# First loads on the weights' queue, two more split blocks, and a rearranged last store in a two-layer decoder kernel on one Trainium2 core

## The chip, the core and the metric

The kernel runs on one core of one Trainium2 chip. The metric is device time in microseconds (us) of one execution, lower is better. Before the change it took 2313.56 us (median of three runs, 2311.81 to 2315.46).

## What is computed

Two layers of a decoder trunk over 256 positions with a model width of 2048, all in float32. Layer 0 mixes with a chunked gMLP beside a gated linear recurrence, layer 1 with an attention that forgets; each is followed by a gated MLP (5632 hidden columns) with a causal convolution of width 3 between its up-projection and its activation. Cut to what matters:

```python
for l in range(DEPTH):                                   # DEPTH = 2
    h = rms_norm(x, mix_norm[l])
    h = mixer_ab(h, ...) if l % 2 == 0 else mixer_c(h, ...)
    x = x + h
    h = rms_norm(x, ffn_norm[l])
    x = x + conv_ffn(h, ffn_w_up[l], ffn_conv_w[l], ffn_conv_b[l], ffn_w_down[l])
```

Nearly all of the work is matrix products of the 256 positions with weights that are each read once.

## The kernel before, in words

**Layout.** `x` lies feature-major in SBUF: 16 tiles of 128 features by 256 positions (`xT[0..15]`, L69 to L74), held in seven larger tiles named x0, x1, x2, x4, x6, x8 and x12 after their first index, with 1, 1, 2, 2, 2, 4 and 4 tiles in them. The result leaves in the same layout.

**A product.** [...] `weights` (L145) loads a block `w` of 128x1024 by a DMA on the queue of SyncE (SP), ScalarE (ACT) rounds it to `wh` (L162), VectorE (DVE) forms the rest `wl = w - wh` (L165). The activations are split in the same way into a tile `a` that holds both parts side by side (`split`, L272; from x by `Norm.feed_split`, L317: ACT writes the high part, DVE the low one). Each pair of tiles then takes three matmuls: high by high, high by low, low by high. There are four buffers for `w`, three each for `wh` and `wl`, and in the later stages a second pool with two more.

**The start.** Layer 0 begins with `project_tok` (L194) for the columns "v": eight blocks of two k-tiles, 12 matmuls of 128x512 each, fed by the weights in order. Nine small matmuls on a tile of ones come first (L135 to L137). `pp` (norm gains and other small parameters; the first 32 columns are needed at once) and x0 are loaded from ACT's queue, x1, x2, x4 and x6 from the queue of GpSimd (POOL) (L81 to L83), x8 and x12 from SP's queue behind the weights of block k = 6 and k = 8 (`FETCH`, L30). For k = 0 and k = 2 the block is loaded and split in two halves (`single`, L154).

**The ends of the stages.** Products that come out position-major go through `transposed` (L247): DVE turns 32x32 blocks within `tmp`, and 16 small DMAs of 32 KB put the blocks into their places in `zt` or `turn`, eight on SP's queue and eight on POOL's, alternating. There are 80 such batches in the kernel. The consumers of a batch are generators in a queue (`tick`, L121); each block of weights advances them one step, and they first let `LAG` = 4 steps pass (3 for the last quarter). So in `add_four` (L368), in `mixer_c` at the queries and keys (L827, consumed at L758), and in the MLP's `four`/`conv` (L887, L903).

**The last stage.** `down` (L972) of layer 1 makes the output in four quarters. For q = 0, 1 and 2 a quarter goes through `add_y` (L945): transpose, wait, add to x (L954), store each tile from SP's queue (L968). The last quarter is made feature-major, one tile m = 12..15 after the other (L975 to L987), added on DVE (L984, L985) and stored. For m = 15 there is no separate eviction (`end`).

**What sets the order.** The Tile framework schedules instructions onto the engines' in-order queues and gives each DMA one of eight completion semaphores for the hardware queues (SP and ACT together) or one of eight for POOL's; a DMA waits until the one that held its semaphore before has landed. `tc.add_manual_dep(..., order)` fixes an order without a semaphore.

Of the kernel before, what the change touches and what calls it, by code (L numbers as in the profile page):

```python
# [12 lines left out]
ALU = mybir.AluOpType  # L13
AX = mybir.AxisListType

P = 128
# [8 lines left out]
BLK = 32  # L25
LAG = 4
WAIT = 4
EPS = 1e-6
WARM = 9
FETCH = {6: (8,), 8: (12,)}  # L30
LANE = 64
LEVELS = (64, 32, 16, 8, 4, 2, 1)
NL = len(LEVELS)
# [2 lines left out]
C_MIX, C_FFN, C_GAM = 0, 32, 64  # L36
# [14 lines left out]
def tile_trunk(ctx: ExitStack, tc: tile.TileContext, x, pp_d, cst_d, mlev_d, msk_d,  # L51
               w_v, w_f, w_g, w_i, w_q, w_u, w_abo, w_cf, w_cqkv, w_cg, w_co, w_up, w_dn, spw_d, spb_d, out):
    nc = tc.nc
    V, SC, PE = nc.vector, nc.scalar, nc.tensor
# [20 lines left out]
    fetch = {c0: (t, c0, n) for t, c0, n in xload}  # L75
# [12 lines left out]
    order = mybir.DependencyInfo(mybir.DependencyClass.NoSync, mybir.DependencyReason.DATA)  # L88
# [15 lines left out]
    def view(ap, off, *dims):  # L104
        return bass.AP(ap.tensor, ap.offset + off, [list(ap.ap[0])] + [list(d) for d in dims])
# [13 lines left out]
    flight, queue = [], []  # L119
# [15 lines left out]
    warm = pm.tile([P, 512], F32, tag="pm", name="warm")  # L135
    for i in range(WARM):
        PE.matmul(warm[:, 0:P], ones, ones, start=True, stop=True)  # L137
# [2 lines left out]
        while flight or queue:  # L140
            tick()

    deep = {"pool": None, "turn": 0}

    def weights(src, n, rows=None, single=None):  # L145
        deep["turn"] += 1
        if deep["pool"] is not None and deep["turn"] > 12 and deep["turn"] % 2:
            pool, nw, ns = deep["pool"], 2, 2
        else:
            pool, nw, ns = wp, 4, 3  # L150
        w = pool.tile([P, n], F32, tag="w", name=nm("w"), bufs=nw)
        wh = pool.tile([P, n], F32R, tag="wh", name=nm("wh"), bufs=ns)
        wl = pool.tile([P, n], F32R, tag="wl", name=nm("wl"), bufs=ns)
        parts = [slice(i, i + n // 2) for i in (0, n // 2)] if single else [slice(0, n)]  # L154
        for p in parts:
            deep["dma"] = nc.sync.dma_start(
                w[:, p] if rows is None else w.rearrange("p (m c) -> p m c", m=rows), src[:, p] if single else src)
        for i, p in enumerate(parts):
# [3 lines left out]
            deep["act"] = SC.activation(wh[:, p], w[:, p], AF.Copy)  # L162
            if deep["turn"] == 5:
                deep["hold"] = deep["act"]
            V.tensor_tensor(wl[:, p], w[:, p], wh[:, p].bitcast(F32), ALU.subtract)  # L165
        return wh, wl
# [27 lines left out]
    def project_tok(wsrc, norm, feed=False):  # L194
        ps = [pm.tile([P, 512], F32, tag="pm", name=nm("pm")) for _ in range(2)]
        k = 0
        for c in (2,) * 8:
            later = []
            if feed:
                for c0 in FETCH.get(k, ()):  # L200
                    t, c0, n = fetch[c0]
                    later.append((t, c0, n))
                if k >= 4:
                    for i in range(c):
                        norm.feed_split(k + i)
            tick()
            wh, wl = weights(wsrc[:, k * 512:(k + c) * 512], c * 512, single=(norm, k) if feed and k < 4 else None)
            for t, c0, n in later:
                r = nc.sync.dma_start(t, x[:, c0:c0 + n, :])
                tc.add_manual_dep(r.ins, deep["dma"].ins.name, order, reason="queue order")  # L210
            if feed and k < 4:
                for i in range(c):
                    a = norm.a[k + i]
                    for j, (o, t) in enumerate(((0, wh), (S, wh), (0, wl))):
                        for T in range(2):
                            PE.matmul(ps[T], a[:, o + T * P:o + (T + 1) * P], t[:, i * 512:(i + 1) * 512],
                                      start=k + i + j == 0, stop=False)
                k += c
                continue
            for T in range(2):  # L220
                for i in range(c):
                    a = norm.a[k + i]
                    ah, al = a[:, T * P:(T + 1) * P], a[:, S + T * P:S + (T + 1) * P]
                    h, l = (t[:, i * 512:(i + 1) * 512] for t in (wh, wl))
                    PE.matmul(ps[T], ah, h, start=k + i == 0, stop=False)  # L225
                    PE.matmul(ps[T], ah, l, start=False, stop=False)  # L226
                    PE.matmul(ps[T], al, h, start=False, stop=k + i == KT - 1)  # L227
            k += c
        return ps
# [14 lines left out]
                    deep['mm'] = PE.matmul(ps[T], al, h, start=False, stop=k + i == n - 1)  # L244
        return ps

    def transposed(src, tmp, dst):  # L247

        for T in range(2):
            V.transpose(tmp.rearrange("p (b m i t) -> p b m i t", b=4, m=4, t=2)[:, :, :, :, T],  # L250
                        src(T).rearrange("p (m b j) -> p b m j", m=4, b=4))
        n = 2 * BLK
        for a in range(4):
            for b in range(4):
                (nc.sync, nc.gpsimd)[(a + b) % 2].dma_start(dst[BLK * b:BLK * (b + 1), :, a * n:(a + 1) * n],  # L255
                                  tmp[BLK * a:BLK * (a + 1), b * 4 * n:(b + 1) * 4 * n]
                                  .rearrange("p (m r) -> p m r", m=4))

# [616 lines left out]
    def ffn(l, norm, last):  # L875
# [5 lines left out]
        nxt = None if last else Norm(C_MIX + KT)  # L881
# [61 lines left out]
        y = hp.tile([P, 2, D], F32, tag="y", name=nm("y"))  # L943

        def add_y(q, finish):  # L945
            tmp, zt = room()
            transposed(lambda T: y[:, T, q * 512:(q + 1) * 512], tmp, zt)

            def rest():
                for _ in range(LAG - (q == 3)):  # L950
                    yield
                for i in range(4):
                    m = 4 * q + i
                    V.tensor_tensor(xT[m], xT[m], zt[:, i], ALU.add)  # L954
                    if finish:
                        finish_x(m)
                    if q < 3 or i % 2:
                        yield
                if q == 3 and not last:
                    for _ in range(WAIT):  # L960
                        yield
                    yield from nxt.finish_tok()

            queue.append(rest())

        def finish_x(m):
            if last:
                nc.sync.dma_start(out[:, m, :], xT[m])  # L968
            else:
                nxt.feed(m)  # L970

        def down(k0, hid, first, final):  # L972
            n = len(hid)
            for q in range(4):
                if last and final and q == 3:  # L975
                    for m in range(4 * q, KT):
                        end = m == KT - 1
                        ps = project(w_dn[l, m], hid, chunks=(n,), k0=k0, run=2, narrow=end)
                        x2 = xT[m].rearrange("p (n t) -> p n t", t=2)
                        if not end:  # L980
                            t = tp.tile([P, S], F32, tag="ev", name=nm("ev"), bufs=3)
                            SC.activation(t.rearrange("p (n t) -> p n t", t=2),
                                          view(ps, S, (1, P), (P, 2)), AF.Copy)
                            V.tensor_tensor(xT[m], xT[m], t, ALU.add)  # L984
                        V.tensor_tensor(x2, x2, view(ps, 0, (1, P), (P, 2)), ALU.add)  # L985
                        finish_x(m)
                    return  # L987
                ps = project_four(w_dn[l, 4 * q:4 * q + 4], hid, n, k0)
                for T in range(2):
                    d = y[:, T, q * 512:(q + 1) * 512]  # L990
                    if first:
                        SC.activation(d, ps[T], AF.Copy)
                    else:
                        V.tensor_tensor(d, d, ps[T], ALU.add)
                if final:
                    add_y(q, True)

        j0, k0, hid = 0, 0, []
        for g, (now, ahead) in enumerate(STEPS):
# [3 lines left out]
            n, final = 4 * now, g == len(STEPS) - 1  # L1003
# [12 lines left out]
    norm = mixer_ab(Norm(C_MIX))  # L1016
    norm = ffn(0, norm, False)
    norm = mixer_c(norm)
# [81 lines left out]
```

## Time and profile before

| | |
|---|---|
| median of three runs | 2313.56 us |
| lowest, highest | 2311.81, 2315.46 us |
| span of the profiled execution | 2312.9 us (its time is recorded as this span only) |
| TensorE busy, share of the span | 2300.0 us, 99% |
| VectorE, ScalarE, GpSimd busy | 67%, 57%, 15% |
| moved by DMA | 481.44 MB, mean 208 GB/s |

How to read it: the profile is of one execution. PE is the TensorE's matmuls and PEld its weight loads; "SPq", "ACTq" and "POOLq" are the engines' DMA-issuing instructions. In a timeline a row has the start, the duration, the engine and line, the operation with output and input, how many instructions are merged in it, and in brackets how long the engine was idle before it and what ended that. "Issue" means that nothing the profile shows was waited for. Matmuls overlap, so a row's duration exceeds its pitch; what a stall costs is read from start to start. In a table of windows there are, for each engine, the busy time and the instructions that started in the window, then the granted TensorE clock (1.00 is full), the DMA share and GB/s.

### The profile page before, as it was taken

How to read it: one execution, taken by the hardware profiler on the slowest of the kernel's cores; microseconds unless marked ns; L12 is line 12 of the kernel's file. 1: busy time of each engine (PE TensorE's matmuls, PEld its weight loads, DVE VectorE, ACT ScalarE, POOL GpSimd, SP SyncE). 2: the span in 40 equal slices, each digit the busy share in tenths (PEclk: the TensorE clock that was granted, in tenths of full speed). 3: DMA queues.
4: the chain of work that ended last, by engine and by line, in shares of the span. 5: the costliest groups of instructions: out<-in, count | busy, mean ns of one | idle time of the engine just before them, and what ended most of it. 6: DMA issues, size and time to landing. Idle time of an engine off the chain costs nothing.

```text
span 2312.9 us, 31358 instructions
## 1 busy us (share of the span) xinstructions
PE 2300.0 (99%) x10354; PEld 1904.7 (82%) x10354; DVE 1559.5 (67%) x2345; ACT 1307.0 (57%) x1958; POOL 350.4 (15%) x650
## 2 busy tenths in 40 slices
PE   9999999999999999999999999999999999999998
PEld 7888888888888888888888888887888888888887
DVE  7677866776566657766866665666776476667766
ACT  7567655665555546654565556655655465455642
POOL 0100112122012002111211101111221022012102
PEclk9999999999999999999999999999999999999999
DMA  8655577777677767776666655777777677667765
GB/s 274 204 161 173 175 218 220 235 235 212 208 210 207 217 196 212 223 216 186 197 230 194 190 182 178 225 221 227 225 219 216 192 218 209 210 205 213 222 206 166
DMA packets 497748, 481.44 MB, mean 208 GB/s; under 512 B 116288, under 2 KB 468688, under 8 KB 497456
## 3 DMA queue, kind: packets, MB, share of 16 engines
q1 hardware_dynamic: 475488, 453.08, 63.9%
q0 software_dynamic: 20944, 24.04, 4.5%
q10 hardware_dynamic: 1152, 2.31, 0.3%
q8 instruction: 81, 1.33, 0.3%
q14 instruction: 83, 0.68, 0.1%
HBM read 435.24 MB, written 2.11 MB: 189 GB/s over the span
## 4 chain that ended last, share of the span: by engine, by line
PE 95%; DVE 1%; DMA 1%; ACT 1%; issue 1%; POOL 0%; SPq 0%; ACTq 0%; DVEq 0%
PE pm L243 26%; PE pm L244 26%; PE pm L242 26%; PE pm L226 5%; PE pm L227 5%; PE pm L225 5%; DVE wl L165 1%; ACT wh L162 0%; PE px L593 0%; DMA w<-in_w_up 0%; PE pm L186 0%; DMA w<-in_w_v 0%; PE px L762 0%; DMA turn<-tmp 0%; PE px L784 0%
## 5 line engine op out<-in xcount | busy, mean ns | idle before, releaser
L165 DVE TENSOR_TENSOR wl<-w,wh 128x1024 fp32r<-128x1024 f32 (+1 forms) x820 | 998.5, 1220 | 647.2 <-ACT wh L162 639.1
L162 ACT ACTIVATE wh<-w 128x1024 fp32r<-128x1024 f32 (+1 forms) x820 | 864.1, 1056 | 797.2 <-PE pm L244 574.4
L242 PE MATMUL pm<-wh,a 128*128 128x512 f32 x1792 | 699.5, 391 | 1.5 <-ACT wh L162 1.5
L243 PE MATMUL pm<-wl,a 128*128 128x512 f32 x1792 | 699.1, 390 | 1.1 <-DVE wl L165 1.1
L244 PE MATMUL pm<-wh,a 128*128 128x512 f32 x1792 | 698.3, 390 | 0.0
L255 POOL DMA_DIRECT2D zt<-tmp x416 | 225.3, 550 | 1206.8 <-DVE tmp L250 1034.6
L243 PEld LDWEIGHTS pm<-wl,a 128*128 128x128 f32 x1792 | 337.0, 188 | 71.8 <-DVE wl L165 2.7
L242 PEld LDWEIGHTS pm<-wh,a 128*128 128x128 f32 x1792 | 336.7, 188 | 71.2 <-ACT wh L162 1.9
L244 PEld LDWEIGHTS pm<-wh,a 128*128 128x128 f32 x1792 | 336.9, 188 | 69.7
L242 PE MATMUL pm<-wh,hid 128*128 128x512 f32 x688 | 267.6, 389 | 0.0
L243 PE MATMUL pm<-wl,hid 128*128 128x512 f32 x688 | 267.6, 389 | 0.0
L244 PE MATMUL pm<-wh,hid 128*128 128x512 f32 x688 | 267.6, 389 | 0.0
L255 POOL DMA_DIRECT2D turn<-tmp x224 | 121.5, 550 | 739.5 <-DVE tmp L250 332.5
L225 PE MATMUL pm<-wh,a 128*128 128x512 f32 x504 | 199.2, 395 | 0.3 <-ACT wh L162 0.3
L226 PE MATMUL pm<-wl,a 128*128 128x512 f32 x504 | 196.5, 390 | 1.5 <-DVE wl L165 1.5
L227 PE MATMUL pm<-wh,a 128*128 128x512 f32 x504 | 196.5, 390 | 0.0
L244 PEld LDWEIGHTS pm<-wh,hid 128*128 128x128 f32 x688 | 129.1, 188 | 26.9
L243 PEld LDWEIGHTS pm<-wl,hid 128*128 128x128 f32 x688 | 129.1, 188 | 26.8
L242 PEld LDWEIGHTS pm<-wh,hid 128*128 128x128 f32 x688 | 129.1, 188 | 26.8
L226 PEld LDWEIGHTS pm<-wl,a 128*128 128x128 f32 x504 | 94.7, 188 | 21.3 <-DVE wl L165 2.1
L225 PEld LDWEIGHTS pm<-wh,a 128*128 128x128 f32 x504 | 94.7, 188 | 20.0 <-ACT wh L162 1.0
L227 PEld LDWEIGHTS pm<-wh,a 128*128 128x128 f32 x504 | 94.7, 188 | 19.8
(214 smaller groups left out, 1828.7 us busy)
## 6 DMA issues: line engine op xcount, KB each, us to landing
w<-in_w_up SPq DMA_DIRECT2D x352, 512.0 KB, 4.6
w<-in_w_dn SPq DMA_DIRECT2D x176, 512.0 KB, 4.5
w<-in_w_cqkv SPq DMA_DIRECT2D x96, 512.0 KB, 4.4
w<-in_w_abo SPq DMA_DIRECT2D x32, 512.0 KB, 4.8
w<-in_w_cg SPq DMA_DIRECT2D x32, 512.0 KB, 4.4
w<-in_w_co SPq DMA_DIRECT2D x32, 512.0 KB, 4.7
zt<-tmp SPq DMA_DIRECT2D x416, 32.0 KB, 2.8
zt<-tmp POOLq DMA_DIRECT2D x416, 32.0 KB, 2.6
```

The lines of the kernel that those rows point to most:

```text
L162: deep["act"] = SC.activation(wh[:, p], w[:, p], AF.Copy)
L165: V.tensor_tensor(wl[:, p], w[:, p], wh[:, p].bitcast(F32), ALU.subtract)
L225: PE.matmul(ps[T], ah, h, start=k + i == 0, stop=False)
L226: PE.matmul(ps[T], ah, l, start=False, stop=False)
L227: PE.matmul(ps[T], al, h, start=False, stop=k + i == KT - 1)
L242: PE.matmul(ps[T], ah, h, start=k + i == 0, stop=False)
L243: PE.matmul(ps[T], ah, l, start=False, stop=False)
L244: deep['mm'] = PE.matmul(ps[T], al, h, start=False, stop=k + i == n - 1)
L255: (nc.sync, nc.gpsimd)[(a + b) % 2].dma_start(dst[BLK * b:BLK * (b + 1), :, a * n:(a + 1) * n], tmp[BLK * a:BLK * (a + 1), b * 4 * n:(b + ...
```

## The change

1. **Start.** pp goes first on SP's queue, x0 and x1 on ACT's. x2, x4 and x6 go on SP's queue, each ahead of the weights of block k = 2, 4 and 6 (`AHEAD`), x8 and x12 behind the weights of k = 6 and k = 8 (`BEHIND`); `in_order` chains all of these, so that the queue holds them in the order of use. POOL issues none of them.
2. **Halves.** The blocks k = 4 and k = 6 are loaded and split in halves too (eight half blocks in all), with the matmul order of the halves.
3. **Warm-up.** Eight small matmuls instead of nine.
4. **End, transposes.** The 16 small DMAs of the last batch (q = 2) are dealt to three queues, SP 6, ACT 5, POOL 5; they were dealt to SP 8 and POOL 8.
5. **End, adds.** The four adds of that quarter come two steps after their transposes and without steps between them, after an earlier tile's sum; the sum of m = 15 is put behind them.
6. **End, stores.** The tiles are stored in larger pieces: m = 4 and 5 in one transfer and m = 12 to 14 in one transfer from SP's queue, m = 6 and 7, m = 8 to 11 and m = 15 from ACT's. There were 16 stores of 128 KB on SP's queue, now there are nine.

Cut to its core:

```diff
-WARM = 9
-FETCH = {6: (8,), 8: (12,)}
+WARM = 8
+AHEAD = {2: 2, 4: 4, 6: 6}
+BEHIND = {6: 8, 8: 12}
...
-    SC.dma_start(pp[:, 0:C_FFN], pp_d[:, 0:C_FFN])
-    for i, (t, c0, n) in enumerate(xload[:5]):
-        (nc.gpsimd if i else SC).dma_start(t, x[:, c0:c0 + n, :])
+    SC.dma_start(*fetch[0])
+    first_dma = nc.sync.dma_start(pp[:, 0:C_FFN], pp_d[:, 0:C_FFN])
+    SC.dma_start(*fetch[1])
...
+    def in_order(r):
+        tc.add_manual_dep(r.ins, deep["dma"].ins.name, order, reason="queue order")
+        deep["dma"] = r
...
+        for i, p in enumerate(parts):
+            if single and i == 0 and single[1] in AHEAD:
+                in_order(nc.sync.dma_start(*fetch[AHEAD[single[1]]]))
...
-                if k >= 4:
+            if feed and k >= 8:
...
-            wh, wl = weights(wsrc[:, k * 512:(k + c) * 512], c * 512, single=(norm, k) if feed and k < 4 else None)
+            wh, wl = weights(wsrc[:, k * 512:(k + c) * 512], c * 512, single=(norm, k) if feed and k < 8 else None)
+            if feed and k in BEHIND:
+                in_order(nc.sync.dma_start(*fetch[BEHIND[k]]))
...
-                (nc.sync, nc.gpsimd)[(a + b) % 2].dma_start(dst[BLK * b:BLK * (b + 1), :, a * n:(a + 1) * n],
+                qs = queues or (nc.sync, nc.gpsimd)
+                qs[(a + b) % len(qs)].dma_start(dst[BLK * b:BLK * (b + 1), :, a * n:(a + 1) * n],
...
+            end = last and finish and q == 2
+            transposed(lambda T: y[:, T, q * 512:(q + 1) * 512], tmp, zt,
+                       (nc.sync, SC, nc.gpsimd) if end else None)
             def rest():
-                for _ in range(LAG - (q == 3)):
+                for _ in range(2 if end else LAG - (q == 3)):
                     yield
                 for i in range(4):
                     m = 4 * q + i
-                    V.tensor_tensor(xT[m], xT[m], zt[:, i], ALU.add)
+                    r = V.tensor_tensor(xT[m], xT[m], zt[:, i], ALU.add)
+                    if end:
+                        deep["early"] = r
+                        tc.add_manual_dep(r.ins, deep["sum"].ins.name, order, reason="after an earlier sum")
                     if finish:
                         finish_x(m)
-                    if q < 3 or i % 2:
+                    if (q < 3 or i % 2) and not end:
                         yield
...
-            if last:
+            if not last:
+                nxt.feed(m)
+            elif m in (7, 11):
+                t = xload[4 if m == 7 else 5][0]
+                n = 2 if m == 7 else 4
+                SC.dma_start(out[:, m + 1 - n:m + 1, :], t)
+            elif m < 4:
                 nc.sync.dma_start(out[:, m, :], xT[m])
-            else:
-                nxt.feed(m)
+            elif m == 5:
+                nc.sync.dma_start(out[:, 4:6, :], xload[3][0])
+            elif m == 14:
+                nc.sync.dma_start(out[:, 12:15, :], xload[6][0][:, 0:3])
+            elif m == 15:
+                SC.dma_start(out[:, 15, :], xT[15])
...
-                        V.tensor_tensor(x2, x2, view(ps, 0, (1, P), (P, 2)), ALU.add)
+                        r = V.tensor_tensor(x2, x2, view(ps, 0, (1, P), (P, 2)), ALU.add)
+                        if end:
+                            tc.add_manual_dep(r.ins, deep["early"].ins.name, order, reason="last")
+                        deep["sum"] = r
                         finish_x(m)
```

More of the change, by code (lines that the diff above doesn't have):

```diff
@@ L74, in tile_trunk @@
         xT += [t[:, i] for i in range(n)]
-    fetch = {c0: (t, c0, n) for t, c0, n in xload}
+    fetch = {c0: (t, x[:, c0:c0 + n, :]) for t, c0, n in xload}
     pp = cp.tile([P, -(-NPP // LANE) * LANE], F32, tag="pp", name="pp")
@@ L197, in project_tok @@
         for c in (2,) * 8:
[L198 to L202, printed above, removed]
-                if k >= 4:
-                    for i in range(c):
-                        norm.feed_split(k + i)
-            tick()
-            wh, wl = weights(wsrc[:, k * 512:(k + c) * 512], c * 512, single=(norm, k) if feed and k < 4 else None)
[L208 to L211, printed above, removed]
+            if feed and k >= 8:
+                for i in range(c):
+                    norm.feed_split(k + i)
+            tick()
+            wh, wl = weights(wsrc[:, k * 512:(k + c) * 512], c * 512, single=(norm, k) if feed and k < 8 else None)
+            if feed and k in BEHIND:
+                in_order(nc.sync.dma_start(*fetch[BEHIND[k]]))
+            if feed and k < 8:
                 for i in range(c):
@@ L245, in project_four, with transposed @@
         return ps
-    def transposed(src, tmp, dst):
+    def transposed(src, tmp, dst, queues=None):
         for T in range(2):
```

9 lines of the change are left out of this document (5 added, 4 removed).

## The prediction

> **What bounds the kernel now.** I read the page's busy times and chain first, then TensorE's rows for its few stalls, then what each stall waited for, back to its DMA.
>
> ```profile
> PE 2300.0 (99%) x10354; PEld 1904.7 (82%) x10354; DVE 1559.5 (67%) x2345; ACT 1307.0 (57%) x1958; POOL 350.4 (15%) x650
> 15.41 0.23 PE pm L226
> ```
>
> TensorE is busy for 99%, and the chain of waits gives a 128x512 matmul a pitch of 0.23 us. The change adds and removes no matmul but one of the warm-up. So it can only touch the start, the end, and stalls between, which the busy share hides because a stalled matmul's row is long. TensorE's timeline has them:
>
> ```profile
> 5.47 1.63 PE L216 MATMUL pm<-wh,a 128*128 128x512 f32 x4 [0.20 <-DVE a L288]
> 6.94 0.63 PE L216 MATMUL pm<-wl,a 128*128 128x512 f32 x2
> 13.74 0.50 PE L226 MATMUL pm<-wl,a 128*128 128x512 f32 x1 [0.76 <-DVE wl L165]
> ...
> 1234.79 0.39 PE L227 MATMUL pm<-wh,a 128*128 128x512 f32 x1
> 1235.47 0.50 PE L225 MATMUL pm<-wh,a 128*128 128x512 f32 x1 [0.29 <-ACT wh L162]
> 1236.73 0.50 PE L226 MATMUL pm<-wl,a 128*128 128x512 f32 x1 [0.76 <-DVE wl L165]
> ...
> 1599.59 0.39 PE L244 MATMUL pm<-wh,a 128*128 128x512 f32 x1
> 1601.45 0.50 PE L242 MATMUL pm<-wh,a 128*128 128x512 f32 x1 [1.48 <-ACT wh L162]
> 1602.71 0.50 PE L243 MATMUL pm<-wl,a 128*128 128x512 f32 x1 [0.76 <-DVE wl L165]
> ```
>
> Start to start, less two pitches: at 1235 1.94 - 0.46 = 1.5 us are lost, at 1600 3.12 - 0.46 = 2.7 us. The row at 13.74 is the 26th matmul of the first product: 25 pitches are 5.75 us, it came 8.27 us after the first, so the start loses 2.5 us; 0.55 of it in the first four, which take 1.47 us to the row at 6.94 (a clock not yet granted), 1.95 in waits. The granted clock follows the stall at 1600:
>
> ```profile
> 0.00:3.07 3.07, 2.01 (x9) 2.01 (x10) 0.17 (x2) 1.28 (x1) 1.98 (x8) 1.00 0.36 98
> 3.07:6.48 3.41, 3.21 (x14) 2.75 (x13) 1.47 (x4) 1.34 (x3) 0.52 (x1) 1.00 1.00 327
> 1600.50:1603.90 3.40, 1.69 (x6) 1.20 (x7) 3.31 (x6) 3.40 (x5) 0.00 (x0) 1.00 0.37 112
> 1603.90:1607.30 3.40, 3.40 (x10) 2.65 (x9) 2.49 (x4) 1.67 (x3) 0.00 (x0) 0.50 0.88 263
> ```
>
> After 1.69 us busy out of 3.40 the clock is 0.50 for 3.4 us, in which TensorE does what takes 1.7 us at full clock. So it costs up to 1.7 us; I count 1.5.
>
> **The change, part by part. First what it does to POOL**, far from the lines it edits. ACT and DVE waited at both stalls for small transposing DMAs issued by POOL:
>
> ```profile
> 1233.53 0.93 ACT L758 ACTIVATE qk<-turn,gq 128x256 f32<-128x256 f32 x2 [5.42 <-DMA w<-in_w_cqkv]
> 1597.70 1.10 DVE L378 TENSOR_TENSOR x<-x,turn 128x256 f32<-128x256 f32 x3 [3.53 <-DMA w<-in_w_up]
> 1220.23 5.11 SPq L255 DMA_DIRECT2D turn<-tmp  x8
> 1223.11 4.37 POOL L255 DMA_DIRECT2D turn<-tmp  x8 [45.41 <-issue]
> 1585.33 1.63 POOL L255 DMA_DIRECT2D turn<-tmp  x3 [17.42 <-DVE tmp L250]
> 1589.35 2.71 POOL L255 DMA_DIRECT2D turn<-tmp  x5 [2.39 <-issue]
> 1590.28 12.78 SPq L156 DMA_DIRECT2D w<-in_w_up  x6
> 2304.12 0.55 POOL L255 DMA_DIRECT2D zt<-tmp  x1 [2.09 <-issue]
> ```
>
> (The releaser named is a weight load, because it shares the wait; the input, `turn`, tells.) POOL pauses for over 2 us with nothing to wait for: before the batch at 1223.11 (2.9 us behind SP's half), within that at 1585, and before the very last at 2304.12. Windows cut at the pauses show a rule; the last POOL number counts its instructions, all DMAs:
>
> ```profile
> 1.20:445.00 443.80, 441.72 (x2051) 364.11 (x2051) 323.79 (x641) 285.26 (x542) 61.44 (x113) 1.00 0.68 209
> 445.00:858.00 413.00, 412.61 (x1821) 341.34 (x1820) 265.10 (x346) 224.06 (x290) 57.42 (x106) 1.00 0.71 211
> 858.00:1223.10 365.10, 364.93 (x1642) 302.83 (x1641) 259.58 (x387) 202.99 (x298) 57.98 (x107) 1.00 0.69 210
> 1223.10:1589.00 365.90, 364.85 (x1675) 303.63 (x1674) 237.56 (x334) 210.03 (x326) 58.01 (x107) 1.00 0.66 200
> 1589.00:1943.00 354.00, 351.76 (x1546) 290.56 (x1545) 232.99 (x316) 202.63 (x272) 57.41 (x106) 1.00 0.72 216
> 1943.00:2304.00 361.00, 361.00 (x1606) 299.29 (x1604) 237.69 (x314) 181.65 (x230) 57.40 (x106) 1.00 0.69 205
> ```
>
> 113 DMAs, then 106 or 107, then a pause, each time: POOL runs out of something that is refilled. Four of the first 113 are the x loads of L83, which the change takes away. If an x load counts as one of the small ones, each pause comes four small DMAs later. Counting batches of eight from 0, the pauses move from batch 13 (after 5 of 8), 26 (7), 40 (0), 53 (3), 66 (5) and 79 (7) to 14 (1), 27 (3), 40 (4), 53 (7) and 67 (1); the sixth would need six more DMAs than are left, as three of the last batch also go to ACT's queue.
>
> [...]
>
> *Batch 53.* SP's weight loads start at 1590.28. Of POOL's queue (q0) the table of queues has (packets, MB, share) in the window 1592.4 to 1596.6
>
> ```profile
> q0 software_dynamic: 96, 0.10, 7.1%
> ```
>
> and in that of 1228.4 to 1232.3, at batch 40:
>
> ```profile
> q0 software_dynamic: 96, 0.10, 7.5%
> ```
>
> 0.10 MB are three transfers of 32 KB, so among the weights each takes 1.4 us (1.3 in batch 40), hence DVE at 1597.70. With seven issued ahead of the pause one is left: issued near 1591.2, done near 1594. DVE and ACT start 2.8 to 3.3 us earlier, which covers the 2.7 us: I take 2.6, and 1.5 for the clock, which then has no idle window. Bounds: 0 if one DMA lands as late as three, 4.2 for all.
>
> *Batch 40.* POOL starts 2.6 us earlier, pauses after four, and ends 0.3 earlier than now; two DMAs instead of three fall among the weights, the last 1.3 us earlier. ACT's wait holds the `wh` behind it, so it passes on: 1.2 of 1.5 us. Bounds -0.5 (a third is late too) to 1.5.
>
> *Batches 14, 27, 67 for 13, 26, 66.* In 13 the pause made ACT wait, and TensorE lost something:
>
> ```profile
> 451.00 1.09 ACT L910 ACTIVATE conv<-zt,pp 128x256 f32<-128x256 f32 x2 [4.74 <-DMA w<-in_w_up]
> PE pm L243 <- DVE wl L165: 0.4, 1, 0.4
> ```
>
> 26 and 66 cost TensorE nothing: consumers lag four steps. 27 and 67 are second halves of a pair as 13 is. I take two such costs for one: -0.4, bounds -1.5 and +0.4.
>
> **The start.** x came late, from POOL's queue most:
>
> ```profile
> 4.97 0.35 DVE L288 TENSOR_SCALAR a<-x,pp 128x256 fp32r<-128x256 f32 x1 [3.96 <-DMA x<-in_x]
> x<-in_x POOLq DMA_DIRECT2D x3, 256.0 KB, 7.1
> x<-in_x ACTq DMA_DIRECT2D x1, 128.0 KB, 3.7
> ```
>
> Now the halves follow in order of use. At the 327 GB/s of window 3.07:6.48, 256 KB take 0.8 us; a pair of k-tiles with its x (768 KB) takes 2.4 us at most, TensorE 12 x 0.23 = 2.8 us: it does not catch up with the queue. Eight transfers may be in flight, 2 MB or 6 us at that rate, over the 3.7 us that x0 took to land. So the 1.95 us of waits go; the 0.55 us of slow clock stays. The first matmul does not come earlier: in the built order ACT splits x1 ahead of the first `wh`, so it waits for x1 (issued near 1.2 as second on ACT's queue, as x0 was; 3.7 us gives 4.9, less traffic 4.3) + 0.4 + 0.6 = 5.4 us. Against 5.47 that is no gain; I keep 0.15 for small waits. Gain 1.8 (bounds 1.2 to 2.1). The lost warm-up matmul leaves 0.6 us idle ahead of it: nothing, unless the clock reacts (rival C).
>
> **The end.**
>
> ```profile
> 2306.75 0.28 PE L182 MATMUL pm<-hid,wl 128*128 128x256 f32 x1
> 2306.66 1.10 DVE L954 TENSOR_TENSOR x<-x,zt 128x256 f32<-128x256 f32 x3 [1.10 <-DMA out<-x]
> 2308.12 2.28 SPq L968 DMA_DIRECT2D out<-x  x5
> out<-x SPq DMA_DIRECT2D x16, 128.0 KB, 1.8
> ```
>
> TensorE ends at 2307.03; then come the adds that the paused DMA held back, and five stores at 0.46 us each, the last issued near 2310.0, landing 1.8 later, and 1.1 us of closing to 2312.9. Now the last batch's issues end on SP after 6 x 0.64 us, 2301.8, landing near 2303.3 (2 us, a little over the 1.8 of the stores); four adds end near 2304.7; m = 14 near 2305.5; m = 15 is summed at 2307.4, its store issued at once on ACT, landed near 2309.3 to 2309.5. ACT's five issues delay the evictions of m = 12 and 13 to 2302, before the adds need them. Gain 2.4; bounds 1.6 (the 512 KB and 384 KB stores, issued near 2305 to 2306, still move at 270 GB/s when it arrives) and 2.7.
>
> **Sum**: 1.8 + 1.2 + 2.6 + 1.5 - 0.4 + 2.4 = 9.1 us. Against the profiled execution 2312.9 - 9.1 = 2303.8; it stands 0.7 below the median of the runs shown, so I forecast 2304.5.
>
> **Rivals.**
>
> A. As summed, 2304.5, 56%. For it: six pauses fit one count.
>
> B. The pauses move but stay as dear, since the last DMA still lands behind the weights: 1.8 + 2.4 - 0.4, 2309.8. It also holds if the x loads count nothing. For it: in batch 40 the pause only moves from ahead of the first to ahead of the fifth DMA, and the last issue of POOL by 0.3 us. 18%.
>
> C. The clock. It was granted after a window with 3.21 of 3.41 us busy and not after 2.01 of 3.07; now some 2.7 of 3.41. If that is too little, one more window at half clock: 1.7 us more, 2306.2. [...] 12%.
>
> D. The order of use brings nothing at the start, because the eight semaphores hold SP's queue back: 2306.3. 8%.
>
> E. Slower: x1 starves beside SP's stream, as POOL's x tiles did (7.1 us): landing 8.3, first matmul 4.0 us late, and the idle window costs 1.5 of clock. With the pauses as in B that is 2309.8 + 4.0 + 1.5 = 2315.3. It decides from x1 landing after 6.6 us: 2.3 late and 1.5 of clock are the 3.8 that B gains. Against it: x0 took 3.7 with more traffic. 6%.
>
> **How the numbers follow.** About 0.2% (4.6 us, below 2308.9) is what a measurement can tell from no change. A, C and D lie below; a quarter of B does, the rest is "same"; E is slower but for its small values. With a little for what I do not see: faster 0.77, same 0.16, slower 0.07. The range holds A with its bounds, C, D and most of B: 2301.5 to 2310.0.
>
> **What would show it.** Right: windows cut at POOL's pauses count x113, x106, x107, x107, x106 again, all small DMAs, with no pause in the last batch; no TensorE gap near 1597; clock 1.00 there; matmuls without gaps from 5.5 us on; the last store landing 2.5 us after the last matmul. Wrong: a first count of x109 (an x load counts nothing: it is then the fourth DMA of batch 53 that waits), `qk` or `x` still waiting 3 us or more, a clock of 0.50 after 6.5 us, or a first matmul after 6 us.

## The result, and the profile after

| | before | after |
|---|---|---|
| median of the runs | 2314.73 us (7 runs, 2311.81 to 2318.26) | 2308.23 us (7 runs, 2307.11 to 2308.66) |
| ratio, 95% interval | | 0.9973, 0.9963 to 0.9982 |
| span of the profiled execution | 2312.9 us | 2306.1 us (its time: 2308.18) |
| last matmul ends, what follows it | 2307.03, 5.83 us | 2302.56, 3.52 us |

6.5 us faster; forecast were 2304.5 (2301.5 to 2310.0). The profiled executions differ by 6.8 us: 4.47 up to the last matmul, 2.31 behind it. Since both kernels issue the same real matmuls in nearly the same order, one timeline can be laid on the other matmul by matmul. TensorE's timeline of the kernel after, at the places shown of before:

```profile
5.88 0.98 PE L221 MATMUL pm<-wh,a 128*128 128x512 f32 x3 [1.04 <-ACT wh L173]
...
17.12 0.73 PE L230 MATMUL pm<-wh,a 128*128 128x512 f32 x2
18.38 0.50 PE L231 MATMUL pm<-wl,a 128*128 128x512 f32 x1 [0.53 <-DVE wl L176]
...
1233.82 0.41 PE L230 MATMUL pm<-wh,a 128*128 128x512 f32 x1
1235.00 0.50 PE L231 MATMUL pm<-wl,a 128*128 128x512 f32 x1 [0.77 <-DVE wl L176]
...
1598.02 0.50 PE L247 MATMUL pm<-wh,a 128*128 128x512 f32 x1
1599.28 0.50 PE L248 MATMUL pm<-wl,a 128*128 128x512 f32 x1 [0.76 <-DVE wl L176]
...
1975.04 0.39 PE L247 MATMUL pm<-wh,hid 128*128 128x512 f32 x1
1975.74 0.50 PE L248 MATMUL pm<-wl,hid 128*128 128x512 f32 x1 [0.31 <-DVE wl L176]
```

Of the two gaps at each stall of before, the one ahead of `wh` is gone and the one ahead of `wl` is left: 1.18 - 0.23 = 0.95 us at 1235, 1.26 - 0.23 = 1.03 at 1599. A new one of 0.47 stands at 1975.7, and two in the start. The windows of the kernel after, cut where POOL pauses (last pair: POOL's busy time and its DMAs):

```profile
1.20:463.00 461.80, 459.47 (x2129) 378.36 (x2130) 338.97 (x668) 297.78 (x561) 61.39 (x113) 1.00 0.68 210
463.00:877.00 414.00, 414.00 (x1828) 342.82 (x1827) 263.99 (x339) 223.93 (x290) 57.40 (x106) 1.00 0.69 210
877.00:1223.50 346.50, 346.50 (x1561) 287.56 (x1561) 246.15 (x370) 191.18 (x282) 57.95 (x107) 1.00 0.68 209
1223.50:1589.20 365.70, 364.94 (x1677) 303.87 (x1676) 237.60 (x334) 210.50 (x327) 57.92 (x107) 1.00 0.65 201
1589.20:1958.00 368.80, 368.05 (x1625) 304.53 (x1624) 245.93 (x334) 213.33 (x288) 57.39 (x106) 1.00 0.72 219
```

The counts are those of before, 113, 106, 107, 107, 106, and each falls four small DMAs later, in the batches named: 14, 27, 40, 53, 67. An x load counts as one.

### The profile page after: what moved, and what is told of

Its sections match the earlier page's. It is cut to its first block, busy times and chain, and to the rows that moved or that the text cites. A ratio compares the mean times of both kernels' runs of the same rounds, so it can differ in the third digit from the quotient of the medians.

```text
span 2306.1 us, 31359 instructions
## 1 busy us (share of the span) xinstructions
PE 2297.3 (100%) x10352; PEld 1902.7 (83%) x10352; DVE 1559.2 (68%) x2347; ACT 1306.3 (57%) x1960; POOL 346.4 (15%) x643
## 4 chain that ended last, share of the span: by engine, by line
PE 95%; ACT 1%; DVE 1%; DMA 1%; issue 1%; SPq 0%; POOL 0%; ACTq 0%; DVEq 0%
PE pm L248 26%; PE pm L249 26%; PE pm L247 26%; PE pm L231 4%; PE pm L232 4%; PE pm L230 4%; ACT wh L173 1%; PE pm L221 0%; PE px L599 0%; PE pm L197 0%; SPq L261 0%; DVE wl L176 0%; DMA zt<-tmp 0%; PE px L768 0%; DMA turn<-tmp 0%
## 5 line engine op out<-in xcount | busy, mean ns | idle before, releaser
L249 PEld LDWEIGHTS pm<-wh,a 128*128 128x128 f32 x1792 | 336.5, 188 | 69.5
L247 PEld LDWEIGHTS pm<-wh,a 128*128 128x128 f32 x1792 | 336.5, 188 | 69.3 <-ACT wh L173 0.3
L916 ACT ACTIVATE conv<-zt,pp 128x256 f32<-128x256 f32 x176 | 95.4, 589 | 25.3 <-DMA zt<-tmp 18.5
L232 PEld LDWEIGHTS pm<-wh,a 128*128 128x128 f32 x496 | 93.2, 188 | 19.4
```

The source lines that it names most:

```text
L916: SC.activation(c, z, AF.Identity, bias=pp[:, cb:cb + 1], scale=w(2))
```

## The experiments

Twelve kernels. "Before beside it" is the kernel before on the same chip in the same hours.

| run | median (range), runs | before beside it | ratio, 95% interval |
|---|---|---|---|
| start_only | 2310.67 (2309.47 to 2311.43), 10 | 2314.02 | 0.9981, 0.9971 to 0.9990 |
| end_only | 2312.42 (2310.42 to 2320.29), 10 | 2314.02 | 0.9998, 0.9989 to 1.0008 |
| extra4 | 2309.22 (2308.67 to 2313.30), 10 | 2314.02 | 0.9980, 0.9970 to 0.9989 |
| extra27 | 2310.78 (2309.03 to 2313.28), 10 | 2314.02 | 0.9987, 0.9978 to 0.9997 |
| parked | 2306.75 (2304.88 to 2307.43), 5 | 2314.77 | 0.9966, 0.9953 to 0.9979 |
| start_order | 2308.29 (2306.68 to 2309.59), 6 | 2314.77 | 0.9972, 0.9960 to 0.9984 |
| warm10 | 2308.02 (2307.62 to 2309.18), 7 | 2314.77 | 0.9970, 0.9958 to 0.9981 |
| end2q | 2310.79 (2308.77 to 2312.31), 10 | 2314.77 | 0.9984, 0.9974 to 0.9993 |
| start_kept | 2310.71 (2308.84 to 2314.44), 10 | 2314.83 | 0.9983, 0.9974 to 0.9993 |
| before_parked | 2308.20 (2306.99 to 2311.56), 10 | 2314.83 | 0.9975, 0.9966 to 0.9985 |
| parked_all | 2304.72 (2304.44 to 2305.18), 4 | 2314.83 | 0.9960, 0.9945 to 0.9975 |
| parked_start | 2305.45 (2304.09 to 2305.77), 5 | 2314.96 | 0.9955, 0.9941 to 0.9969 |

Where the profiled executions gained against that of before, in us: by how much less time passed between two matmuls around each place (the same two in both timelines), and behind the last one. "Attention" is a stretch at 1184 to 1205 us in which the profiled execution of before lost 0.3 to 0.5 us more than any other, with the change and without it.

| | start, to the 1800th matmul | batch 13 | 26, 27 | attention | 40 | 53 | clock after 53 | 67 | behind the last |
|---|---|---|---|---|---|---|---|---|---|
| after | +0.2 | +0.7 | -0.2 | +0.5 | +0.5 | +1.6 | +1.7 | -0.6 | +2.3 |
| start_only | 0.0 | +0.7 | -0.3 | +0.3 | +0.7 | +1.2 | +1.7 | -0.7 | +0.3 |
| end_only | -0.1 | +0.7 | 0.0 | +0.5 | -0.2 | -0.3 | +1.7 | 0.0 | +2.0 |
| extra4 | -0.3 | +0.7 | 0.0 | +0.3 | +0.6 | +0.5 | 0.0 | 0.0 | +2.0 |
| parked | +1.3 | +0.7 | -0.6 | +0.5 | +1.6 | +2.8 | +1.7 | 0.0 | +2.2 |
| parked_all | +1.2 | +0.7 | 0.0 | +0.5 | +1.6 | +2.8 | +1.7 | 0.0 | +2.1 |
| before_parked | +0.1 | -3.7 | 0.0 | +0.5 | +1.6 | +2.8 | +1.7 | 0.0 | +0.6 |

### Halves of the change: start_only and end_only

The first has the change's start (first loads, `AHEAD`, `BEHIND`, half blocks, `WARM = 8`) in the kernel before, the second its end (`queues`, adds, stores).

> The kernel before with the start of the change alone (first loads, half blocks, eight warm-up matmuls); the end stays as before. Theory 1 (the four x loads that leave POOL's queue move POOL's pauses, and that alone moves the stalls in the middle): all of the 4.5 us that the last matmul comes earlier is there, the pauses fall at DMA 113, 219, 326, 433, 539 of POOL and none in the last batch (642 DMAs in all, the sixth would be ahead of the 646th), so about 1.2 us of the end go too: near 2309.0 us. Theory 2 (the middle was gained by something else, and the start is worth what it shows by 60 us, 0.3): near 2314.4 us.

Measured 2310.67. POOL's pauses stand where the whole change has them, and nearly all of its gain in the middle is there: theory 1. Two sizes were off: the last matmul came 3.65 us earlier and not 4.5, and the end gave 0.3 for the missing pause and not 1.2.

> The kernel before with the end of the change alone (last batch on three queues, adds, larger stores). Theory 1: POOL's first five pauses stand where they stood before (batches 13, 26, 40, 53, 66), the stalls at 459, 1235 and 1600 us with the clock at 0.50 after them are all there, the sixth pause is gone since POOL issues 643 DMAs: 2.3 us from the end, near 2312.4 us. Theory 2: part of the 4.1 us of the middle comes with it, 2308 to 2311 us.

Measured 2312.42, as theory 1 had it (1.6 us below the kernel before beside it, where 2.3 were expected); the pauses are the old ones. The profiled execution (2310.42) is the shortest of the ten, and shows something else: the stall at 1600 is there, but not the half clock behind it. Its timeline and, with the phase of its clock, its windows; then the windows of extra4, next to be told:

```profile
1598.75 0.39 PE L244 MATMUL pm<-wh,a 128*128 128x512 f32 x1
1600.86 0.49 PE L242 MATMUL pm<-wh,a 128*128 128x512 f32 x1 [1.72 <-ACT wh L162]
1602.12 0.50 PE L243 MATMUL pm<-wl,a 128*128 128x512 f32 x1 [0.77 <-DVE wl L165]
```

```profile
1597.67:1601.08 3.41, 1.69 (x8) 1.07 (x6) 3.33 (x10) 3.41 (x8) 0.00 (x0) 1.00 0.04 13
1601.08:1604.50 3.42, 2.65 (x11) 1.99 (x11) 3.42 (x5) 2.35 (x4) 0.00 (x0) 1.00 0.70 214
```

```profile
1597.71:1601.13 3.42, 1.69 (x7) 0.87 (x6) 3.33 (x8) 3.42 (x8) 0.00 (x0) 1.00 0.09 19
1601.13:1604.54 3.41, 3.41 (x9) 2.63 (x10) 2.82 (x4) 2.23 (x3) 0.00 (x0) 0.50 0.81 258
```

1.69 us busy in a window of 3.4 left the clock at 1.00 in one execution and halved it in the other. So the clock is a lottery whose odds a stall sets: nine of end_only's ten runs have a mean clock under 1.000, of the change's 7 none. (Of the 77 runs of before beside these experiments 75 have, but there the mean takes in more of the idle end: in the profiled one the clock is 0.50 in its last 2.4 us too.)

### The pauses put back: extra4, extra27

In both, n DMAs of 32 bytes per partition that nobody reads go on POOL's queue near 20 us.

```diff
         fetch_late(wt[1], spb_d.partition_broadcast(P))
+        for j in range(EXTRA):
+            nc.gpsimd.dma_start(extra[:, 8 * j:8 * j + 8], cst[:, 0:8])
```

> The changed kernel with four tiny extra DMAs on POOL's queue near 20 us (32 bytes per partition, nobody reads them), in number what the x loads were. Theory 1: a pause is set by the count of DMAs alone, whatever their size, so the pauses return to batches 13 (after 5 of 8), 26 (7), 40 (0), 53 (3) and 66 (5), none at the end, and TensorE loses again 1.5 us at 1235, 2.7 at 1600 and 1.6 by the clock, 0.5 at 459, and wins 0.5 at 1975: 4.1 us more, near 2312.3 us. Theory 2 (the stalls have another cause): no difference, 2308.2 us.

Measured 2309.22, 1.0 above the change and not 4.1. (The intervals of the two ratios overlap; no run of extra4 lies below the change's slowest, 2308.66.) The pauses did go back, to batches 13, 26, 40, 53 and 66, with DMAs of 4 KB that nobody waits for: the count is one of DMAs, not of bytes. What they cost was mis-sized. Seven of its ten runs keep the clock at 1.000 (2308.67 to 2310.71), three do not (2311.25, 2312.14, 2313.30; the profiled one is the first of these); batch 40 cost no more than after four more DMAs (0.6 and 0.5 of gain in the table); and batches 27 and 67 are given back, 0.8 us. Batch 53's stall costs 1.64 - 0.50 = 1.1 us more than in the change, so 0.3 of the medians' 1.0 is accounted for. In the profiled pair 0.5 at the start (the clock was granted at 10.5 us and not at 5.5) and 0.3 behind the last matmul come to it; what does in the other runs isn't shown.

> The same with 27 extra DMAs. Theory 1: the pauses come at batches 10 (after 6 of 8), 24 (0), 37 (2), 50 (3), 63 (5) and 76 (7), and the stalls behind batches 40, 53 and 67 (0.95, 1.03 and 0.53 us) are gone; what the pauses cost in the new batches lies between nothing (batches 14 and 27 cost nothing) and as much again: 2305.7 to 2308.2 us. Theory 2: the stalls at 1234 and 1598 us stay, 2308.2 us or more.

Measured 2310.78: slower than the change, where I had expected the same or less. The stalls at 1235, 1600 and 1975 are gone, as theory 1 says. But the pauses now fall in batches 10, 37 and 50, and there they cost 1.0, 1.9 and as much again by a half clock, and 2.2 us. TensorE behind batch 50:

```profile
1535.15 0.39 PE L251 MATMUL pm<-wh,yc 128*128 128x512 f32 x1
1536.57 0.50 PE L249 MATMUL pm<-wh,yc 128*128 128x512 f32 x1 [1.03 <-ACT wh L175]
1537.83 0.50 PE L250 MATMUL pm<-wl,yc 128*128 128x512 f32 x1 [0.76 <-DVE wl L178]
```

The shape is that of before at 1600: one gap ahead of `wh`, then 1.26 from `wh` to `wl`. So 53 is no special batch; but a pause can also be free (24, 63 and 76 here).

### The pauses taken out: parked, parked_all, before_parked

If the pause comes by count, a DMA that nobody waits for can take it. `park` puts a few such DMAs behind a batch, when POOL is idle:

```diff
+PARK = {39: 6, 52: 3, 65: 2, 78: 2}
...
+        batch["n"] += 1
+        if batch["n"] != 40:
+            park(last)
```

(for batch 39 behind cb's broadcast; parked_all has {13: 3, 26: 1, 39: 2, 52: 3, 65: 2, 78: 2}, before_parked {39: 2, 52: 3, 65: 2, 78: 2} in the kernel before.)

> The changed kernel with thirteen tiny DMAs on POOL's queue in idle places: six ahead of batch 40 (behind the broadcast of cb), three ahead of 53, two ahead of 66 and two ahead of 79, counted so that each pause from the third on falls on one of them and no batch has one. Theory 1 (a stall is the pause's own): the waits at 1234, 1598 and 1975 us (0.95, 1.03 and 0.53 us) are gone and nothing takes their place, 2.5 us less than the changed kernel's 2308.2: near 2305.7 us. Theory 2 (what makes those batches late is the weight loads around them, and the pause only adds to it): a part of each stall stays, 2307 to 2308 us.

> The changed kernel with thirteen tiny DMAs so dealt that all six pauses fall on one of them (ahead of batches 14, 27, 40, 53, 66 and 79). In the run parked the pause within batch 27 cost 0.47 us at 892 us, in the changed kernel nothing. Theory 1: no wait over 0.3 us is left between 65 us and the last matmul, 0 to 0.5 us less than parked's 2306.75: near 2306.4 us. Rival (pauses in layer 0's MLP are covered by the four steps between a batch and its use, the 0.47 was the weights'): as parked, 2306.75 us.

> The kernel before with nine tiny DMAs on POOL's queue in idle places (two ahead of batch 40, three ahead of 53, two ahead of 66, two ahead of 79) and nothing else: start, end and queues as before. Theory 1 (the stalls behind batches 40 and 53 and the clock that falls after the second belong to the pauses): 1.5 + 2.7 us less for the last matmul, and 1.6 more in executions whose clock would have fallen, and 0.3 at the end (the adds no longer wait for the paused DMA): 2314.7 - 4.5 to 6.1 = 2308.6 to 2310.2 us, as much as the whole change brings. Theory 2: the batches are late without a pause too, a gain under 1.5 us.

Measured 2306.75, 2304.72 and 2308.20. POOL's timeline of parked_all at batch 53, and its windows:

```profile
1566.45 1.10 POOL L259 DMA_DIRECT2D extra<-cst  x2 [1.97 <-issue]
1581.34 4.37 POOL L273 DMA_DIRECT2D turn<-tmp  x8 [13.79 <-DMA w<-in_w_up]
```

```profile
446.00:857.00 411.00, 411.00 (x1815) 340.33 (x1814) 265.35 (x346) 223.62 (x289) 57.60 (x106) 1.00 0.71 211
857.00:1177.00 320.00, 320.00 (x1422) 265.24 (x1422) 230.21 (x336) 177.34 (x247) 58.14 (x107) 1.00 0.70 210
1177.00:1566.00 389.00, 389.00 (x1807) 324.77 (x1806) 252.22 (x363) 224.85 (x361) 58.15 (x107) 1.00 0.65 201
1566.00:1914.50 348.50, 348.50 (x1541) 288.64 (x1540) 231.58 (x312) 200.92 (x271) 57.61 (x106) 1.00 0.73 219
```

The pause of 2 us stands ahead of the second of the tiny DMAs, 15 us before the batch, whose eight go out in one run of 4.37 us. In every window TensorE is busy for the whole of it. This is theory 1 without a rest: no stall was the weights' own, and parked_all has the lowest median of the study, 3.5 us under the change (no run of the one reaches the other). It is 1.7 us lower than I had expected; the profiled executions of parked and parked_all differ by 0.4 us only, so most of what lies between their medians isn't explained. Nine tiny DMAs in the kernel before bring 6.6 us, as much as the whole change and more than the 4.5 to 6.1 expected. In its profiled execution the pause within batch 13, which was left, cost 2.6 us and the clock, against 0.5 in before and nothing in extra4 in the same place, so that price is a lottery too:

```profile
458.46 0.39 PE L244 MATMUL pm<-wh,a 128*128 128x512 f32 x1
461.31 0.50 PE L245 MATMUL pm<-wl,a 128*128 128x512 f32 x1 [2.46 <-DVE wl L167]
```

That parked's pause in batch 27 cost 0.6 (gone in parked_all) and the change's 0.2 belongs to it.

### The start: start_order, start_kept, parked_start, warm10

The start of the kernel after is 2.0 us ahead by the 26th matmul (11.72 against 13.74) and 0.6 by the 156th. Its ACT timeline, and from the issues by line x8's load (512 KB, us to landing), there issued at 7.61, in before at 3.87:

```profile
14.41 1.71 ACT L292 ACTIVATE a<-x,pp 128x256 fp32r<-128x256 f32 x4 [0.65 <-DMA x<-in_x]
16.02 1.04 ACT L173 ACTIVATE wh<-w 128x1024 fp32r<-128x1024 f32 x1
```

```profile
x<-in_x SPq DMA_DIRECT2D x1, 512.0 KB, 6.8
```

```profile
x<-in_x SPq DMA_DIRECT2D x1, 512.0 KB, 10.0
```

x8 lands at 14.4 (before 13.9): sorting the queue by use brings the first tiles earlier, and the last of the same bytes no earlier. TensorE, now ahead, waits for it: landing, four splits of 0.40, `wh` 1.04, `wl` 1.23 give 18.3, the row at 18.38.

```diff
+                    if k >= 10 and deep["turn"] < 8:
+                        tc.add_manual_dep(deep["split"].ins, deep["act"].ins.name, order, reason="behind wh")
```

(and the same for the split of x1.)

> The changed kernel with two orders on ACT: the high part of the first half block ahead of the split of x1, and the high parts of the blocks k = 8 and k = 10 ahead of the splits of the x tiles of the next block (now four splits stand ahead of each). Theory S (the start gains 2.0 us by the 26th matmul and gives 1.4 back because ACT's splits hold the weights of the blocks k = 8 and 10): the first matmul comes near 5.3 instead of 5.9, the waits at 17.5 and 21.0 us go; the last matmul comes 1.4 to 2.0 us earlier, near 2306.5 us. Rival (what comes late there is the data, x8 at 14.4 us and the weights behind it): the waits move by a few matmuls and stay as long, 2308.2 us.

Measured 2308.29, no gain, though the waits of the start went and the 156th matmul came 1.3 us earlier (41.50 against 42.77). (The first came at 5.82 and not 5.3; x1 landed at 5.3 in this execution.) DVE's timeline and TensorE's behind it:

```profile
44.69 0.63 DVE L459 CAST msk<-kst 128x896 bf16<-128x896 f32 x1 [3.16 <-DMA kst<-in_msk]
45.23 0.15 DVE L307 TENSOR_SCALAR rm<-px 128x2 f32<-128x2 f32 x1
```

```profile
50.40 0.39 PE L251 MATMUL pm<-wh,a 128*128 128x512 f32 x1
51.34 0.50 PE L252 MATMUL pm<-wl,a 128*128 128x512 f32 x1 [0.56 <-DVE wl L178]
```

DVE stands 3.2 us for kst, the last of the late loads, with the norm's numbers behind it. Loading kst second of the late loads instead:

> The changed kernel with the two orders on ACT of the run start_order and, besides, the load of kst (the masks, 448 KB on ACT's queue) as second of the late loads instead of last. In start_order the first eight blocks ended 1.3 us earlier than in the changed kernel (156th matmul at 41.50 against 42.77 us), and it was lost at 50 and 57 us, after DVE had stood 3.2 us for kst (landed 44.67, 41.0 before the change). Theory K (the gain of the start is given back to the late loads, of which kst is the last): the stalls at 50 and 57 us go and the last matmul comes 1.2 us earlier than in the changed kernel, near 2307.0 us. Rival (another wait of that stage takes the place, the gate's loads or the norm's numbers): the 1.2 us are lost again before 65 us, 2308.2 us.

2310.71: worse. The wait only moved: DVE then stood for the gate's weights at 34.2 (1.31 us), and TensorE 2.95 - 0.23 = 2.7 us at 36.65. Leaving the loads and moving DVE's cast behind the norm's numbers, on parked_all:

```diff
-        V.tensor_copy(msk, kst)
+        r = V.tensor_copy(msk, kst)
+        tc.add_manual_dep(r.ins, deep["rsq"].ins.name, order, reason="behind the norm")
```

> All six pauses on tiny DMAs as in parked_all, the two orders on ACT of start_order, and the cast of the masks (msk from kst) on DVE behind the norm's numbers instead of ahead of them. In start_order the 156th matmul ended the start at 41.50 us (parked_all 42.14), and 1.2 us were lost at 50 and 57 us, after DVE stood 3.2 us for kst with the norm queued behind. Theory K2 (a late load gives the start's gain back only by what is queued behind its consumer on DVE): the cast still starts when kst has landed, but no wait follows at 50 and 57 us, and the 1800th matmul comes 0.6 us earlier than in parked_all (391.66): near 391.0 us, the whole near 2304.1 us. Rival (something else of that stage holds it): 391.6 us or later, 2304.7 us or more.

kst landed as late (44.1), no wait followed at 50 and 57, and the 1800th matmul came 0.5 us earlier than in parked_all (391.14 against 391.66, by the expectation's count): theory K2. The median, 2305.45, doesn't differ from parked_all's 2304.72 by more than the ranges; the profiled executions have 2304.09 and 2304.44.

> The changed kernel with ten warm-up matmuls in place of eight, so that TensorE idles 0.2 us ahead of the first product and not 1.0. Theory W (the clock is granted after a window of 3.41 us with more than 2.7 us busy, at a phase that differs from execution to execution; in the traces so far 2.64 was not enough and 2.79 was; the hole of 1.0 us costs those executions in which it lies in the first full window): granted before 8 us, and the median up to 1 us lower, 2307.2 to 2308.2 us, with the highest time of the runs lower too. Rival (the grant doesn't depend on the hole): no difference; if the two more delay the first product, up to 0.3 us more.

2308.02, no difference that can be told (`WARM = 10`). Theory W isn't borne out: its profiled execution idled 0.7 us ahead of a first matmul at 6.40, and a window with 2.72 us busy, which ended at 7.0, brought no grant: that came at 10.4. In parked_all a window with 2.71, which ended at 5.55, did bring it.

### The third queue: end2q

```diff
-                       (nc.sync, SC, nc.gpsimd) if end else None)
+                       None)
```

> The changed kernel with the last batch on two queues again (SP 8, POOL 8), the rest of the end as changed. POOL issues 642 DMAs, so no pause there. Theory E (the end's 2.3 us come from fewer stores in a row and from the adds that no longer stand behind the last sum; the third queue is spare time): adds 1 us later but still done before the last sum, 2308.2 to 2308.6 us. Rival (the third queue brings the earlier adds and with them the earlier last stores): 1 to 2 us of the end are lost, 2309.2 to 2310.2 us.

2310.79, the rival: 5.39 us behind the last matmul and not 3.52. DVE's timeline and ACT's stores:

```profile
2303.62 1.43 DVE L962 TENSOR_TENSOR x<-x,zt 128x256 f32<-128x256 f32 x4 [0.30 <-issue]
2304.97 0.41 DVE L1006 TENSOR_TENSOR x<-x,pm 128x256 f32<-128x256 f32 x1
```

```profile
2305.08 0.35 ACTq L983 DMA_DIRECT2D out<-x  x1
2305.53 0.39 ACTq L991 DMA_DIRECT2D out<-x  x1
```

With two queues the built order has the four adds behind the sum of m = 14 and not ahead of it, so the last sum and two stores come behind them. (0.7 of the 1.9 us lie behind the last landing, in the closing; the rest of its loss against the change, in TensorE, is mostly a start with the clock granted only at 12.5 us.)

## Why the prediction was right, and where it was not

**The mechanism** held: POOL's pauses come by a count of DMAs, moved to the batches named, and the stalls behind them shrank. An x load, which writes 128 partitions, and a DMA of a batch, which writes 32, count alike: the first pause comes after x113 with four x loads among them (before) and with none (after). The forecast had assumed this; no run of before showed it. 6.8 us of 9.1 came, and 0.5 of these ("attention") are luck, which no term of the sum had. Forecast and median differ by 3.7 us: 2.3 of this, 1.1 of the base, and 0.3 outside the span. With its base set right, the forecast of A would lie 2.6 us below the median and B's time 2.7 above it: the mechanism was A's, the size half-way to B.

**The base: 1.1 us.** "It stands 0.7 below the median of the runs shown": that compared a span with a time. The 77 runs of before that list both have a time 1.8 us above their span, so the profiled execution took about 2314.7, and the forecast would have been 2314.7 - 9.1 = 2305.6. (The changed kernel's runs lie 2.1 above theirs; these 0.3 us, outside the span, I can't explain.)

**The start: 1.8 forecast, 0.2 measured.** The step that failed is "it does not catch up with the queue". The 26th matmul came at 11.72, and 5.4 + 25 x 0.23 + 0.55 is 11.7; but that they agree is luck. The first came at 5.88, and from there on the matmuls kept a pitch of 0.23: the 0.55 us of slow clock weren't lost in this execution. The sum of bytes against TensorE's pace was right for these first blocks. It left out x8, a tile of four k-tiles behind 3 MB, and the four splits that ACT takes ahead of the block's weights. Of the 0.6 us that were left, 0.2 were lost at 60 us, behind a wait of DVE for kst (1.73 us, to 44.53), and 0.2 in smaller pieces. And x1 landed at 4.7 and not 4.3, so the first matmul came 0.4 later than before. With the same start code parked and parked_all kept 1.2 to 1.3 us: in them x8 landed at 13.6 and 13.8, and kst (parked) at 42.1. Rival D had the size of this term, nothing, but for another cause.

**Batch 53: 2.6 forecast, 1.6 measured; batch 40: 1.2 and 0.5.** The step that failed is "one is left: issued near 1591.2, done near 1594". The issue was right (1589.44, on the kernel before's clock 1591.2). The landing was not; issues by line of the kernel after, for seven of batch 53 issued ahead of the weights, the last four of batch 40, and the last of batch 53 with a weight load issued 0.3 us ahead of it:

```profile
turn<-tmp POOLq DMA_DIRECT2D x7, 32.0 KB, 1.9
```

```profile
turn<-tmp POOLq DMA_DIRECT2D x4, 32.0 KB, 4.9
```

```profile
turn<-tmp POOLq DMA_DIRECT2D x1, 32.0 KB, 4.7
```

I had read three transfers of 1.4 us in a window as a price per transfer; it is a place in the line. A small DMA lands about when the weight load does that was issued just ahead of it, or within 0.1 us of it: alone in batch 53, 4.7 us after its issue, at 1594.19 (the load at 1594.25); the three of batch 40 after 4.4, 5.3 and 6.3 us, at 1228.78, 1230.17 and 1231.73 (the loads issued at 1224.25, 1224.88 and 1225.48 landed at 1228.60, 1229.91 and 1231.56). There the step that failed is "two DMAs instead of three fall among the weights": POOL's last three went out at 1224.34, 1224.88 and 1225.41, and the first weight load at 1224.25. What waited for the two batches started so, ACT in batch 40 and DVE in batch 53:

```profile
1231.80 0.93 ACT L764 ACTIVATE qk<-turn,gq 128x256 f32<-128x256 f32 x2 [4.89 <-DMA turn<-tmp]
```

```profile
1594.27 1.10 DVE L384 TENSOR_TENSOR x<-x,turn 128x256 f32<-128x256 f32 x3 [1.88 <-DMA w<-in_w_up]
```

The kernel after is 1.20 and 1.79 us ahead there. On the clock of before they started at 1233.00 and 1596.06, 0.5 and 1.6 us earlier than its 1233.53 and 1597.70, and TensorE gained as much. The forecast had 1.3 and 2.8 to 3.3 us; the sign that it named, no gap near 1597, did not come either. Rival B's reason was half right. Whether the small DMA's bytes come late, or only the word of its landing, no run here tells.

**Batches 13, 26, 66: -0.4 forecast, -0.2 measured** (+0.7, -0.2, -0.6), by chance: the same place in batch 13 cost nothing in extra4 and 2.6 us in before_parked.

**The clock: 1.5 forecast, 1.65 measured.** Right in this pair of profiles, and in the medians it is a matter of odds (it fell in nine of ten runs of end_only, which has the stall of before, and in none of the change).

**The end: 2.4 forecast, 2.31 measured**, for a reason that was partly wrong. "The adds that the paused DMA held back": start_only has no pause there and still 5.57 us behind the last matmul. It is the order on DVE, the one queue of stores, and, as end2q shows, the third queue, which I had cost at nothing but an earlier landing. The kernel after, DVE's last sum and the last store:

```profile
2302.60 0.42 DVE L1006 TENSOR_TENSOR x<-x,pm 128x256 f32<-128x256 f32 x1 [1.00 <-PE pm L193]
2303.05 0.34 ACTq L991 DMA_DIRECT2D out<-x  x1
```

**Rival E** came in no run: x1 landed at 4.7 to 5.4 us in all that load it so. **Rival C** did not come in this execution, but in others: in the profiled executions of start_only, end_only, extra4, warm10 and end2q the clock was granted at 9.6 to 12.5 us. The windows of end_only, ten matmuls in the one, 17 in the next (a count takes in those that run into the window):

```profile
7.06:10.47 3.41, 3.41 (x10) 2.64 (x9) 2.53 (x6) 2.14 (x5) 0.00 (x0) 1.00 0.99 387
10.47:13.88 3.41, 3.41 (x17) 2.81 (x15) 2.95 (x7) 3.25 (x6) 0.00 (x0) 1.00 1.02 416
```

**Open.** What the moved pauses alone are worth depends on the clock's odds: extra4 lies 1.0 us above the change by the medians, and 3.0 to 5.1 in the three runs whose clock fell. Why the stall in the old place of batch 53 was 2.2 us in extra4 and 2.7 to 2.9 in before and end_only (each in one execution) was not tried. That POOL runs out of something that is refilled was my reading of the count; no run shows it, only the count and the pause.

## What to carry to other kernels

When an engine issues many DMAs, count them between its unexplained pauses: an edit far away that adds or drops a few can move every later pause, and the time by more than what it was meant for (here four x loads fewer moved five pauses; batches 40 and 53 and the clock gained 0.5, 1.6 and 1.7 us, the start itself 0.2). A pause is best put on a DMA that nobody waits for (parked_all: 2304.72 us against 2308.23). And a small transfer is to be costed by what was queued ahead of it, not by its size (in the kernel after, 32 KB took 1.9 us ahead of the weights, and 4.4 to 6.3 among them).

## What the runs showed of the hardware

- POOL's DMAs pause after 113 and then after each 106 or 107, in the windows of before, after and parked_all; DMAs of 32 bytes per partition (parked_all), 1 KB (the batches') and 2 KB (x2, x4 and x6 in before) count the same. POOL idles 2.09 to 2.50 us there in before and after, 1.97 and 2.50 in two of parked_all's; before's third lies in an idle time of 45.41 us and shows as a start 2.88 us behind SP's half (0.27 in the kernel after).
- A small DMA lands 1.9 us after its issue (1.75 to 1.95 for the seven in the kernel after, batch 53), and after 3.8 to 6.3 with a 512 KB load issued just ahead (batches 40 and 53 of before and after), within 0.7 us of the landing of that load or of one issued within 0.1 us.
- TensorE's clock fell to 0.50 for 3.41 us after a window of 3.41 us with 1.71 us busy (before) and after one with 1.69 (extra4), and stayed at 1.00 after one with 1.69 (end_only). At the start it was granted at 5.47 us (after), 6.48 (before), 10.38 (warm10), 10.47 (end_only) and 10.52 (extra4); the column has 1.00 until then too, but the matmuls tell (end_only: ten in a window, then 17).
- SP's and ACT's DMAs share eight semaphores, POOL's have eight others, and in before and after none of the 2132 and 2127 DMAs was issued before the one that held its semaphore had landed (the x8 load of the kernel after went out at 7.61, the one before it on its semaphore had landed at 7.59).
- A time is 1.8 us above its span in the runs of before, and 2.1 in the change's.
